# Summing the squares of the last two row blocks in halves, and sharing the closing waits between SP and Pool, in an eight-core decoder-trunk kernel

## The chip, the cores and the metric

The kernel runs on all eight cores of one Trainium2 chip (two dies: cores 0 to 3 and 4 to 7), each with its own share of the batch. The metric is the device time of the slowest core, in microseconds (us).

The runs fall into two states. In the fast one all cores are granted nearly the full TensorE clock (0.994 to 0.999 here). In the slow one a die gets less (cores at 0.813 to 0.972 in the slow runs below) and its cores take longer (in the run of squares_only at 1580.22, cores 0 to 3 have 0.861 to 0.879 and take 1559.3 to 1578.6 us, cores 4 to 7 have 0.996 to 0.998 and take 1404.3 to 1408.8).

## The reference

One step of a two-layer decoder trunk. Only its end matters here: the second MLP's output is added to the residual x, and the sum is normalised over its 1024 columns, row by row.

```python
def rmsnorm(x, g):
    xf = x.astype(jnp.float32)
    r = xf * lax.rsqrt(jnp.mean(xf * xf, axis=-1, keepdims=True) + EPS)
    return (r * g.astype(jnp.float32)).astype(x.dtype)
# in trunk(), after the last layer:
#   x = x + jnp.square(jax.nn.relu(h @ ff_w1[l])) @ ff_w2[l]
#   return rmsnorm(x, norm_final), ...
```

## The kernel before

A core holds 2048 rows as 16 row blocks of 128 rows (one row per partition) by 1024 columns. A Python scheduler emits every instruction: generators ("threads") yield operations, and the one that can start earliest goes next; waits between engines follow from the buffers read and written. `ACT(...)` makes a ScalarE activation, `STT` a VectorE scale-and-multiply, `DMA("sp", ...)` a store issued by SP.

The second MLP's output comes from a seven-product (Strassen-like) scheme, on quadrants of two row blocks by two column halves. The last such group handles row blocks 11 and 15. Its results are added to x in the order g (the right halves of both blocks), 11 (left half of block 11), 22 (right half of block 15), 12 (right half of 11), 21 (left half of 15). When a block has had its three additions, its normalisation is started:

```python
            for r in rows:
                b = 4 * (t0 + r) + j
                left[r] -= 1
                if left[r] == 0 and last:
                    if p == pairs[-1]:
                        S.spawn(norm(b, n_out, ("h%d" % n_out, b)), FINPRIO if n_out == 4 else NPRIO)
# ... cut ...
def norm(b, n, done):
    # ... cut: a scratch row ("junk"), and three columns ss, lt, rs of nrm ...
    yield ACT(junk, xb, AF.Square, [Bx], Bj + Bn, accum=ss)          # sum of 1024 squares
    yield ACT(lt, ss, AF.Ln, Bn, Bn, scale=1.0 / 1024, bias=EPS)
    yield ACT(rs, lt, AF.Exp, Bn, Bn, scale=-0.5)                    # 1/sqrt(mean + EPS)
    if n == 4:                                                       # the final norm
        yield up("gfin")
        if b in (14,):
            yield up("lastadd")                  # block 14 waits until the last addition is emitted
        for o, w in ((0, 512), (512, 512)) if b in (11, 15) else ((0, 1024),):
            q = slice(o, o + w)
            # ... cut ...
            yield STT(xb[:, q], xb[:, q], rs, hg[:, q], ALU.mult, ALU.mult, Bq + [Bn, B_hg], Bq)
            # ... cut ...
            yield DMA("sp", xy_ds[b if o == 0 else b - 8], [(yp[b][:, q], x_sb[:, b, q])], Bq, (), 512 * w)
        return
```

So blocks 11 and 15 are squared whole, but scaled and stored in halves of 256 KB. Block 14 is scaled and stored whole, 512 KB. At the end SP waits once for every DMA semaphore that was used (51 of them), in the order in which the scheduler thinks they are met; then all engines meet at the exit (in before between 1410.0 and 1410.2 us):

```python
final_waits = [(d.h, d.count) for d in sorted(P.dsems, key=lambda d: d.t) if d.count > 0]

def make_body(name, final=False):
    def body(eng):
        # ... cut: the engine's own stream ...
        if final:
            for h_, v_ in final_waits:
                eng.wait_ge(h_, v_)
    return body

block.sync(make_body("sp", final=True))
block.gpsimd(make_body("pool"))
```

## Time and profile before

| | before |
|---|---|
| median of the three runs given | 1470.35 us (1411.27 to 1488.31) |
| its fast run | 1411.27 us |
| profiled execution (fast), slowest core | 1410.2 us; all cores 1404.1 to 1410.2 |
| last matmul to the end of the program | 9.18 us on each of the eight cores |

From the page of before (its slowest core, 0): the span; busy time, share of the span and instruction count of each engine; the chain that ended last, by engine.

```profile
span 1410.2 us, 25622 instructions; the slowest of 8 cores (1404.1 to 1410.2 us)
...
PE 1367.9 (97%) x9123; PEld 694.2 (49%) x9145; DVE 1129.6 (80%) x2006; ACT 906.3 (64%) x1825; POOL 185.0 (13%) x265
...
PE 78%; DVE 10%; ACT 6%; DMA 3%; issue 2%; DVEq 0%; SPq 0%; ACTq 0%; POOLq 0%
```

TensorE bounds the kernel (97% of the span, 78% of the chain that ended last). The change touches nothing until the last group of products, so it has to be read in the last ten microseconds. That stretch is the timeline of before (core 0): start, duration, engine, line, operation, out<-in, shapes, count; in brackets the idle time before it and what ended it.

```profile
1399.89 1.88 DVE L564 TENSOR_TENSOR x_sb<-x_sb,pp 128x512 f32<-128x512 f32 x3
...
1400.00 1.02 PE L612 MATMUL pp<-mixT,arena 128*128 128x512 f16 x4
1401.27 1.06 ACT L530 ACTIVATE mixT<-x_sb 128x1024 f16<-128x1024 f32 x1 [1.06 <-DVE x_sb L564]
1401.69 1.28 DVE L582 SCALAR_TENSOR_TENSOR x_sb<-x_sb,nrm,hg 128x1024 f32<-128x1024 f32 x1
1402.23 0.19 ACT L530 ACTIVATION_READ_ACCUMULATOR mixT<-x_sb 128x1 f32 x1
1402.32 1.04 ACT L530 ACTIVATE mixT<-x_sb 128x1024 f16<-128x1024 f32 x1
1403.27 0.19 ACT L530 ACTIVATION_READ_ACCUMULATOR mixT<-x_sb 128x1 f32 x1
1403.36 0.75 ACT L529 ACTIVATE nrm<-nrm 128x1 f32<-128x1 f32 x4
1403.82 2.74 DVE L582 SCALAR_TENSOR_TENSOR x_sb<-x_sb,nrm,hg 128x512 f32<-128x512 f32 x4 [0.85 <-ACT nrm L529]
```

Read it downwards. The last matmuls end at 1401.02 and three additions (22, 12, 21) follow on DVE. ACT had been idle for 1.06 us when it began the first whole square; two squares and four one-column operations then take it to 1404.11. The 1.28 us DVE item in the middle is block 14's scaling; after it DVE idles 0.85 us for ACT, then scales four half rows until 1406.56.

What SP does after its last store (issued at 1406.69, landed at 1408.82) is on no chain in the profile, because waits are not busy time. It shows when one asks for the instructions of the source line of the closing waits (line, engine, count, durations in ns, first and last start):

```profile
L2561 SPq EVENT_SEMAPHORE  x51: 17/17/17, 1407.1 to 1409.9; - x51
```

An instruction takes 17 ns, but 51 of them take 2.88 us: in the trace one starts every 0.05 us, and one takes 0.37. The last is over at 1409.95, 1.13 us after the last landing, and the program ends at 1410.21.

The third thing to read is the store traffic. This is the DMA view of before over 6.00 us that begin 1.60 us after the last matmul (1402.62 to 1408.62): each digit is the busy share of the 16 DMA engines in 0.15 us, in tenths; then the stores with size and median time from issue to landing.

```profile
DMA  0000000049999999910599989999999999989710
...
yp<-x_sb SPq DMA_DIRECT2D x4, 256.0 KB, 2.2
yp<-x_sb SPq DMA_DIRECT2D x1, 512.0 KB, 2.6
```

Block 14's store fills the engines for 1.4 us, a gap of about two digits follows, then the four half-row stores come without a break.

### The profile page before, as it was taken

To read this page: it belongs to the slowest core of one execution; us is meant where nothing else is said; L and a number is where in the kernel's file an instruction comes from. 1 tells how busy PE (TensorE), PEld (TensorE's weight loads), DVE (VectorE), ACT (ScalarE), POOL (GpSimd) and SP (SyncE) were. 2 spreads that over 40 slices of the span, in tenths; PEclk is the share of its full clock that TensorE was granted. 3 is DMA by queue.
4 is the path that set the end of the run, shared out by engine and by line. 5 is a ranking of instruction groups with operands and counts; after the bars stand their busy time and mean duration, and the time that the engine had idled before them with its cause. 6 is when DMAs were issued, how large, how long until landed. Compare 5 with 4: busy or idle time off the path is not lost.

```text
span 1410.2 us, 25622 instructions; the slowest of 8 cores (1404.1 to 1410.2 us)
## 1 busy us (share of the span) xinstructions
PE 1367.9 (97%) x9123; PEld 694.2 (49%) x9145; DVE 1129.6 (80%) x2006; ACT 906.3 (64%) x1825; POOL 185.0 (13%) x265
## 2 busy tenths in 40 slices
PE   7999999999999999999999999999999999999997
PEld 3666655654454444454444444444444544444442
DVE  5897898886687788877778788999768778877777
ACT  5877878874465756854654765466747747745655
POOL 1221134333210110110100000000100100100100
PEclk9999999999999999999999999999999999999999
DMA  8672443397645964865845643630834625754613
GB/s 185 171 127 41 106 112 93 95 205 156 159 82 109 154 109 97 152 114 90 155 93 144 192 154 132 164 71 10 147 60 86 107 45 104 166 106 76 120 30 120
DMA packets 72473, 163.43 MB, mean 116 GB/s; under 512 B 6479, under 2 KB 36398, under 8 KB 72350
## 3 DMA queue, kind: packets, MB, share of 16 engines
q0 software_dynamic: 26960, 90.75, 39.0%
q1 hardware_dynamic: 45246, 70.98, 15.4%
q8 instruction: 76, 1.25, 0.4%
q14 instruction: 47, 0.39, 0.1%
q10 hardware_dynamic: 144, 0.07, 0.0%
HBM read 226.02 MB, written 26.55 MB: 179 GB/s over the span
## 4 chain that ended last, share of the span: by engine, by line
PE 78%; DVE 10%; ACT 6%; DMA 3%; issue 2%; DVEq 0%; SPq 0%; ACTq 0%; POOLq 0%
PE pp L612 40%; PE pp L614 37%; ACT arena L529 3%; DVE mixT L564 2%; PE pp L626 1%; DVE arena L564 1%; ACT pp L529 1%; DMA ring<-w2w 1%; DMA x_sb<-xp 1%; DVE x_sb L564 1%; DVE arena L582 1%; DVE hT L564 1%; DVE x_sb L570 1%; DVE arena L1845 1%; DMA ring<-wst 1%
## 5 line engine op out<-in xcount | busy, mean ns | idle before, releaser
L529 ACT ACTIVATE pp<-pp 128x512 f32<-128x512 f32 x456 | 260.0, 582 | 287.8 <-PE pp L612 194.5
L564 DVE TENSOR_TENSOR x_sb<-x_sb,pp 128x512 f32<-128x512 f32 (+1 forms) x392 | 293.8, 778 | 93.8 <-ACT pp L529 41.7
L614 PE MATMUL pp<-hT,ring 128*128 128x512 f16 (+1 forms) x1460 | 253.4, 311 | 4.5 <-DMA ring<-wst 1.7
L529 ACT ACTIVATE arena<-arena 128x512 f16<-128x512 f16 (+1 forms) x285 | 173.8, 625 | 23.9 <-DVE arena L1845 15.3
L529 ACT ACTIVATE arena<-pp 128x512 f32<-128x512 f32 (+2 forms) x224 | 131.1, 588 | 50.2 <-PE pp L614 29.3
L614 PEld LDWEIGHTS pp<-hT,ring 128*128 128x128 f16 x1460 | 108.9, 97 | 110.3 <-issue 9.5
L612 PE MATMUL pp<-hT,ring 128*128 128x512 f16 x648 | 159.9, 379 | 1.3 <-ACT pp L529 1.1
L612 PE MATMUL pp<-ring,arena 128*128 128x512 f16 x512 | 130.5, 379 | 0.8 <-ACT pp L529 0.8
L612 PEld LDWEIGHTS pp<-hT,ring 128*128 128x128 f16 x648 | 62.2, 98 | 77.1 <-issue 5.6
L614 PE MATMUL pp<-ring,mixT 128*128 128x512 f16 x416 | 96.8, 379 | 1.3 <-DVE mixT L564 1.2
L612 PE MATMUL pp<-mixT,arena 128*128 128x512 f16 x368 | 92.6, 379 | 0.0
L1845 DVE CUSTOM_DVE_ANT_0 arena<-pp,ring 128x512 f16<-128x512 f32 x106 | 70.1, 686 | 24.7 <-ACT pp L529 15.0
L612 PEld LDWEIGHTS pp<-ring,arena 128*128 128x128 f16 x512 | 49.5, 98 | 60.0 <-issue 1.9
L530 ACT ACTIVATE arena<-x_sb 128x1024 f16<-128x1024 f32 x56 | 59.0, 1054 | 21.6 <-DVE x_sb L564 18.2
L564 DVE TENSOR_TENSOR arena<-arena 128x1024 f16<-128x1024 f16 (+2 forms) x100 | 62.7, 648 | 11.1 <-ACT arena L529 10.2
L614 PE MATMUL pp<-ring,hT 128*128 128x128 f16 (+2 forms) x960 | 66.7, 226 | 0.1
L612 PE MATMUL pp<-mixT 128*128 128x512 f16 x240 | 61.6, 379 | 3.9 <-ACT pp L529 3.9
L529 ACT ACTIVATE x_sb<-x_sb 128x512 f32<-128x512 f32 (+3 forms) x98 | 54.1, 559 | 14.1 <-DVE x_sb L564 10.2
L614 PEld LDWEIGHTS pp<-ring,hT 128*128 128x128 f16 (+1 forms) x960 | 60.0, 97 | 5.4 <-issue 0.5
L614 PE MATMUL pp<-mixT,arena 128*128 128x512 f16 x240 | 61.4, 379 | 0.7 <-DVE arena L564 0.7
L612 PE MATMUL pp<-ring 128*128 128x512 f16 x240 | 61.6, 379 | 0.0
L612 PE MATMUL pp<-hT,mixT 128*128 128x512 f16 x240 | 61.6, 379 | 0.0
(266 smaller groups left out, 2312.7 us busy)
## 6 DMA issues: line engine op xcount, KB each, us to landing
ring<-w2w POOLq DMA_DIRECT2D x50, 512.0 KB, 8.4
ring<-w1w POOLq DMA_DIRECT2D x45, 512.0 KB, 8.6
ring<-wsc SPq DMA_DIRECT2D x24, 896.0 KB, 5.8
ring<-wst POOLq DMA_DIRECT2D x41, 512.0 KB, 8.6
x_sb<-xp SPq DMA_DIRECT2D x28, 512.0 KB, 5.7
extra<-w1w POOLq DMA_DIRECT2D x15, 512.0 KB, 7.8
yp<-x_sb SPq DMA_DIRECT2D x14, 512.0 KB, 2.8
x_sb<-st_hgrn SPq DMA_DIRECT2D x24, 256.0 KB, 4.3
```

Source lines behind the costliest of these rows:

```text
L529: return e.activation(out=out, in_=in_, func=func, bias=bias, scale=scale)
L530: return e.activation(out=out, in_=in_, func=func, bias=bias, scale=scale, accum_out=accum)
L564: return Op(eng, lambda e: e.tensor_tensor(out=out, in0=in0, in1=in1, op=op), R, W, *span(0.066, 0.15, n, two))
L570: return Op(eng, lambda e: e.tensor_tensor(out=out, in0=in0, in1=in1, op=op), R, W, occ, occ + 0.08)
L582: return Op("dve", lambda e: e.scalar_tensor_tensor(out=out, in0=in0, scalar=scalar, in1=in1, op0=op0, op1=op1), R, W, *(span(0.068, 0.218 ...
L612: ins = e.matmul(o, l, r, start=s, stop=t, skip_group_check=True)
L614: ins = e.matmul(o, l, r, start=s, stop=t)
L626: ins = e.transpose(out=o, in_=i, identity=idn)
L1845: yield Op("dve", lambda e: e._custom_dve(TENSOR_ADD_SAT, out=v, in0=bank(k), in1=gst(n), s0=3e38, s1=0.0), [B_ps[k], B_gst[n % 2]], B, 0. ...
```

## The change

Two ideas for the close. (1) Each of blocks 11 and 15 has one half complete early (11 after product "11", 15 after "22"). Its squares can be summed then, in time in which ACT is idle; only the other half remains after the last additions. The first half's sum, already divided by 1024 and with EPS added, becomes the bias of the later Ln. (2) SP keeps only the nine waits for the DMA semaphores expected last; Pool, which has no work left by then (in before its last issue ends at 1356.55), takes the other 42.

```diff
+NEND = 9
-        def norm(b, n, done):
+        def norm(b, n, done, parts=None):
 ...
-            yield ACT(junk, xb, AF.Square, [Bx], Bj + Bn, accum=ss)
-            yield ACT(lt, ss, AF.Ln, Bn, Bn, scale=1.0 / 1024, bias=EPS)
+            bias = EPS
+            if parts is not None:
+                bias = nrm[:, 4 * k + 3:4 * k + 4]
+                q = slice(parts * 512, parts * 512 + 512)
+                yield ACT(junk[:, q], xb[:, q], AF.Square, [Bx[parts]], Bj + Bn, accum=ss)
+                yield ACT(bias, ss, AF.Copy, Bn, Bn, scale=1.0 / 1024, bias=EPS)
+                yield up(("xsum", b))
+                q = slice(512 - parts * 512, 1024 - parts * 512)
+                yield ACT(junk[:, q], xb[:, q], AF.Square, [Bx[1 - parts]], Bj + Bn, accum=ss)
+            else:
+                yield ACT(junk, xb, AF.Square, [Bx], Bj + Bn, accum=ss)
+            yield ACT(lt, ss, AF.Ln, Bn, Bn, scale=1.0 / 1024, bias=bias)
             yield ACT(rs, lt, AF.Exp, Bn, Bn, scale=-0.5)
 ...
+                            end = last and n_out == 4 and p == pairs[-1] and j == 3
+                            if end and what in ("11", "22"):
+                                S.spawn(norm(b, n_out, None, h), FINPRIO)
 ...
-                                if left[r] == 0 and last:
+                                if left[r] == 0 and end:
+                                    flags.add(("xsum", b))
+                                elif left[r] == 0 and last:
 ...
-        final_waits = [(d.h, d.count) for d in sorted(P.dsems, key=lambda d: d.t) if d.count > 0]
+        used_sems = sorted((d for d in P.dsems if d.count > 0), key=lambda d: d.t)
+        final_waits = {"pool": used_sems[:-NEND], "sp": used_sems[-NEND:]}
 ...
-                if final:
-                    for h_, v_ in final_waits:
-                        eng.wait_ge(h_, v_)
+                for d in final_waits.get(name, ()):
+                    eng.wait_ge(d.h, d.count)
```

More of the change, by code (lines that the diff above doesn't have):

```diff
@@ L2541, in build, with make_body @@
         S.run()
-        final_waits = [(d.h, d.count) for d in sorted(P.dsems, key=lambda d: d.t) if d.count > 0]
-        def make_body(name, final=False):
+        used_sems = sorted((d for d in P.dsems if d.count > 0), key=lambda d: d.t)
+        final_waits = {"pool": used_sems[:-NEND], "sp": used_sems[-NEND:]}
+        def make_body(name):
             def body(eng):
@@ L2558, in body @@
                         ins.then_inc(P.esem[name], 1)
-                if final:
-                    for h_, v_ in final_waits:
-                        eng.wait_ge(h_, v_)
+                for d in final_waits.get(name, ()):
+                    eng.wait_ge(d.h, d.count)
             return body
-        block.sync(make_body("sp", final=True))
+        block.sync(make_body("sp"))
         block.scalar(make_body("act"))
```

## The prediction

> **What bounds the kernel now.** TensorE: busy 97% of the 1410.2 us span, 78% of the chain that ended last (the page). The change touches only the close. On every core the last matmul ends 9.18 us before the program (timelines). Slowest core, us from the span's start:
>
> - 1401.02 last matmul; the last adds end at 1400.58 (22), 1401.17 (12), 1401.77 (21).
> - ACT squares row block 11 whole (1401.27, 1.06 us), then 15 (1402.32, 1.04); the last Exp ends at 1404.11.
> - DVE's four half-row scalings start at 1403.82, every 0.66 us, and end at 1406.56.
> - SP's last store: issued 1406.69, landed 1408.82.
> - From 1407.07 to 1409.95 SP runs 51 closing waits, one per 0.05 us (one takes 0.37). The program ends at 1410.21, 0.26 us after the last wait and 1.39 us after the last landing (eight cores: 1.24 to 1.41).
>
> **Closing waits.** SP keeps nine; Pool, idle since 1356, takes 42, whose latest landing is at about 1391. SP then needs 9 x 0.05 = 0.45 us (estimate), done before the last landing. After the landing remain one wait's reaction and the 0.26 us exit: 0.31 instead of 1.24 to 1.41. Gain **0.95 to 1.1 us**, all critical: the list of waits outlasts the transfer beside it. [...]
>
> **Squares in halves.** For each of two row blocks two 128x512 squares replace one whole, with one more accumulator read and a 128x1 copy (about 0.19 us each, as the trace's Ln). [...] The first halves mostly go into ACT's 1.06 us of idle before 1401.27. After the add at 1401.17 ACT has two halves to do, not two wholes, plus copies: the first scaling starts 0.5 to 0.9 us earlier (DVE is busy with block 14 until 1402.9).
>
> **But the stores eat most of it.** A half-row store (256 KB) keeps the 16 DMA engines busy for 0.70 us, and scalings come every 0.66: the DMA view shows the engines full from 1405.6 to 1408.3. Block 14's store before them (1403.93 to 1405.35) doesn't move, as its scaling waits for the last add. Between it and the first half-row store the engines idle only 0.32 us: the last landing comes **about 0.3 us** earlier.
>
> **Total: 1.3 us** (0.9 to 1.7): last matmul to end 9.18 -> about 7.9; span 1410.2 -> about 1408.9; fast state 1411.3 -> **1410.0 us**. Fast runs should fall in 1406 to 1414. Two of the three runs before were slow (1470, 1488); a median may be slow again, so the range on record, 1406 to 1480, spans both. Chances: faster 0.01, same 0.97, slower 0.02.
>
> **Right or wrong in the profile.** Right: nine waits end SP; the end follows the last landing by about 0.3 us; first scaling 0.5 to 0.9 us earlier against the last matmul, last landing only 0.3; no DMA idle between the last five stores. Wrong: the landing moves as far as the scaling (stores not the limit), or not at all.
>
> **What would make it wrong.** The first half-square delays the PSUM copy that the last product waits for (1399.28), delaying the last matmul; the extra copies' waits on their own engine eat the ACT gain; Pool's waits or exit come last.

The sum: 0.95 to 1.1 us from the closing waits and about 0.3 us from the landing, 1.3 us in all (0.9 to 1.7). In after a half square takes 0.61 to 0.63 us of ACT.

## The result, and the profile after

Ratios here are the mean time of one kernel's fast runs over that of the other's of the same rounds, so they are not quite the ratios of the medians beside them.

| | before | after |
|---|---|---|
| runs | 1470.35, 1488.31, 1411.27, 1411.23 | 1410.80, 1409.99, 1409.41, 1410.93 |
| median of all | 1440.81 us | 1410.39 us |
| states | two slow, two fast | all fast |
| ratio of fast runs | | 0.9993, 95% interval 0.9969 to 1.0017: same |
| last matmul to end, eight cores | 9.18 (all) | 7.74 to 8.02, median 7.79 us |

The timeline of after (slowest core, now core 4, last matmul at 1401.45):

```profile
1400.31 0.61 ACT L531 ACTIVATE mixT<-x_sb 128x512 f16<-128x512 f32 x1
1400.31 1.88 DVE L565 TENSOR_TENSOR x_sb<-x_sb,pp 128x512 f32<-128x512 f32 x3
...
1400.43 1.02 PE L613 MATMUL pp<-mixT,arena 128*128 128x512 f16 x4
...
1401.09 0.63 ACT L531 ACTIVATE mixT<-x_sb 128x512 f16<-128x512 f32 x1
1401.63 0.19 ACT L531 ACTIVATION_READ_ACCUMULATOR mixT<-x_sb 128x1 f32 x1
1401.72 0.19 ACT L530 ACTIVATE nrm<-nrm 128x1 f32<-128x1 f32 x1
1402.00 0.63 ACT L531 ACTIVATE mixT<-x_sb 128x512 f16<-128x512 f32 x1
...
1402.96 0.61 ACT L531 ACTIVATE mixT<-x_sb 128x512 f16<-128x512 f32 x1
...
1403.79 2.74 DVE L583 SCALAR_TENSOR_TENSOR x_sb<-x_sb,nrm,hg 128x512 f32<-128x512 f32 x4 [0.40 <-ACT nrm L530]
```

Four half squares now. The first (1400.31) and the second (1401.09), with block 14's Exp moved between them (1400.92), fill what was idle time: the second ends 0.27 us after the last matmul, and before's idle ended 0.25 after it. The third starts at 1402.00, although its addition ended at 1401.60: the small copy at 1401.72, which empties the sum's column, stands before it. DVE's wait before the scalings fell from 0.85 to 0.40 us, and they start 2.34 us after the last matmul (1403.79 - 1401.45), not 2.79 (1403.82 - 1401.02).

The closing waits of after, and its DMA view over the same 6.00 us counted from its own last matmul (1403.05 to 1409.05):

```profile
L2577 POOLq EVENT_SEMAPHORE  x42: 17/17/17, 1356.4 to 1391.2; - x42
L2577 SPq EVENT_SEMAPHORE  x9: 17/17/17, 1407.0 to 1408.9; - x9
```

```profile
DMA  0000000049999999988999899989998999970000
...
yp<-x_sb SPq DMA_DIRECT2D x4, 256.0 KB, 2.3
yp<-x_sb SPq DMA_DIRECT2D x1, 512.0 KB, 2.9
```

Pool is done with its 42 waits at 1391, long before the end. SP's last three waits now really wait, each for a store to land: the ninth passes at 1408.92, when the last store lands (1408.90), and the program ends at 1409.19. The gap between block 14's store and the half-row stores is gone. The train starts in the same digit and ends about two digits earlier, less than the scalings' 0.45 us: the stores queue (2.3 and 2.9 us to landing, before 2.2 and 2.6).

### The profile page after: what moved, and what is told of

Same layout as the page of the kernel before. It is cut to its first block, busy times and chain, and to the rows that moved or that the text cites. A ratio compares the mean times of both kernels' runs of the same rounds, so it can differ in the third digit from the quotient of the medians.

```text
span 1409.2 us, 25632 instructions; the slowest of 8 cores (1402.6 to 1409.2 us)
## 1 busy us (share of the span) xinstructions
PE 1368.0 (97%) x9123; PEld 694.1 (49%) x9145; DVE 1128.9 (80%) x2006; ACT 906.5 (64%) x1831; POOL 185.1 (13%) x265
## 4 chain that ended last, share of the span: by engine, by line
PE 80%; DVE 10%; ACT 5%; DMA 2%; issue 2%; DVEq 0%; SPq 0%; POOL 0%; ACTq 0%; POOLq 0%
PE pp L613 40%; PE pp L615 38%; ACT arena L530 3%; DVE mixT L565 2%; PE pp L627 1%; DVE arena L565 1%; ACT pp L530 1%; DVE x_sb L565 1%; DMA ring<-wst 1%; DVE arena L583 1%; DVE hT L565 1%; DVE x_sb L571 1%; DVE x_sb L583 1%; DMA x_sb<-xp 1%; DVE arena L1856 1%
## 5 line engine op out<-in xcount | busy, mean ns | idle before, releaser
L613 PE MATMUL pp<-mixT 128*128 128x512 f16 x240 | 61.6, 379 | 3.7 <-ACT pp L530 3.7
L615 PE MATMUL pp<-mixT 128*128 128x512 f16 x240 | 61.6, 379 | 0.0
```

What stands on the lines that cost most here:

```text
L613: ins = e.matmul(o, l, r, start=s, stop=t, skip_group_check=True)
L615: ins = e.matmul(o, l, r, start=s, stop=t)
```

## The experiments

For a change of about 1 us the whole time is a poor measure: fast runs of one kernel spread over 1 to 3 us (after_again 1410.03 to 1411.50, before beside after_again 1411.71 to 1414.40). So I measured from the last matmul to four later events in each profile. The issue times repeat to 0.02 us over cores and runs. Landings differ between the two cores of a pair (0 and 1, 2 and 3, 4 and 5, 6 and 7): in every profile here, the core of a pair with the longer span (the slower core; the slowest of them sets the time) landed sooner relative to its last matmul (in after 7.45 to 7.52 us against 7.49 to 7.73). "Landing" and "end" in this table are medians over the slower core of each pair; the median of all eight cores, which the expectations speak of, is in brackets. Why the two differ was not tested.

| us after the last matmul | first scaling of 11 | last issue | last landing | end |
|---|---|---|---|---|
| before | 2.79 | 5.67 | 7.78 (7.84) | 9.18 (9.18) |
| close_only | 2.79 | 5.67 | 7.77 (7.87) | 8.06 (8.16) |
| squares_only | 2.34 | 5.21 | 7.46 (7.48) | 8.73 (8.73) |
| after | 2.34 | 5.21 | 7.47 (7.50) | 7.76 (7.79) |
| after_again | 2.34 | 5.21 | 7.49 (7.53) | 7.78 (7.82) |
| keep30 | 2.34 | 5.21 | 7.47 (7.49) | 7.76 (7.78) |
| keep45 | 2.34 | 5.21 | 7.46 (7.53) | 8.43 (8.43) |
| nocopy | 2.09 | 4.96 | 7.47 (7.48) | 7.76 (7.77) |
| split14 | 2.34 | 5.21 | 7.32 (7.34) | 7.61 (7.63) |
| both | 2.09 | 4.96 | 7.08 (7.21) | 7.37 (7.50) |

All eight runs gave correct results, and all profiles are of the fast state. The first four ran on one chip, the second four on another. Two questions: does the end follow the later of landing and list of waits (against: gains simply add up, wait by wait)? And do the stores limit the landing (against: the landing follows the scalings at a fixed distance)?

### close_only: the waits shared, the squares whole

```diff
 # before, with this part of the change alone
+used_sems = sorted((d for d in P.dsems if d.count > 0), key=lambda d: d.t)
+final_waits = {"pool": used_sems[:-NEND], "sp": used_sems[-NEND:]}
```

> Before with the closing waits alone split (SP keeps nine, Pool takes the rest); the squares stay whole. Measured from the last matmul to the end of the program, which was 9.18 us on all eight cores before and 7.74 to 8.02 after. My theory (the end is the later of two chains beside each other, the last store's landing and SP's list of waits): the last landing stays where it was before, 7.60 to 7.94 us after the last matmul by core (7.80 on the slowest), and the end follows 0.29 us after it: 8.05 to 8.25. Rival (the halved squares bring nearly all of the gain, the list hides under the transfer): 9.0 to 9.2. Whole time: 0.07% against before, not to be told from noise; slow runs, if any, fall on either kernel.

Measured: scaling, issue and landing as before; the end on the eight cores 8.05 to 8.27 us after the last matmul, 0.29 after the landing. The closing alone brings 0.91 to 1.13 us. (The expectation has a slip: the cores of before land at 7.77 to 7.94, not 7.60 to 7.94. Those of close_only land at 7.76 to 7.98, and so the latest end is 0.02 over the range expected.) Its source line shows why (slowest core): nine waits on SP, the last of them at the landing.

```profile
L2562 SPq EVENT_SEMAPHORE  x9: 17/17/17, 1406.7 to 1408.4; - x9
```

Whole time: ratio 0.9991, interval 0.9976 to 1.0006, same (medians 1409.99 against 1411.71, all 4 and 7 runs fast).

### squares_only: the squares in halves, the old closing

```diff
 # after, with SP waiting 51 times again
-final_waits = {"pool": used_sems[:-NEND], "sp": used_sems[-NEND:]}
+final_waits = [(d.h, d.count) for d in sorted(P.dsems, key=lambda d: d.t) if d.count > 0]
```

> After with the old closing: SP alone waits 51 times. My theory: the scalings and the last store's issue come 0.45 us earlier than before, as in after, the last landing only about 0.34 earlier; but the list of waits runs from the issue, so here the end follows the issue: 0.45 us earlier than before, 9.18 -> 8.73. So the two halves of the change, 1.0 and 0.45 apart, bring less than their sum together (1.16 to 1.44 by core). Rival (parts add, each acts on the landing): end 0.34 earlier, 8.84. Second rival (halves do nothing): 9.18.

Measured: 8.72 to 8.74 on all cores, as the list theory said; the additive rival's 8.84 is out. The end came 0.45 us earlier, the landing 0.32 (over all eight 0.36, by the table). The whole gain of the issue (0.46 by the table) passed on to the end, because SP's list starts at the issue and outlasts the landing (slowest core: landing at 1408.10):

```profile
L2576 SPq EVENT_SEMAPHORE  x51: 17/17/17, 1406.2 to 1409.1; - x51
```

So the parts are worth 1.12 and 0.45 alone and 1.42 together (all from the table): once the closing is shared, the half squares add 0.30. Of its four runs two were slow (1580.22 and 1540.12, one die at a clock of 0.861 to 0.912); its fast runs took 1410.95 and 1410.79.

### keep30 and keep45: how many waits are free

```diff
-NEND = 9
+NEND = 30        # keep45: 45
```

> After with 30 waits left to SP instead of nine. My theory: 30 x 0.05 = 1.5 us of waits start 0.38 us after the last issue and are done before the landing 2.2 to 2.5 us after it: last matmul to end as in after, 7.74 to 8.02 us, 0.29 us after the landing. Rival (each wait that SP keeps costs its share of the gain, 1.05 us / 42 = 0.025 us): 0.5 us more than after, about 8.3.

> After with 45 waits left to SP. My theory: 45 x 0.05 = 2.25 us, with the one slow wait seen before (0.37) 2.6, plus 0.38 ahead of it: SP is done 2.6 to 3.0 us after the last issue, later than the landing (2.2 to 2.5). End 8.1 to 8.4 us after the last matmul, the same on every core, not tied to the landing. Rival (0.025 us for each wait): 0.9 us more than after, 8.6 to 8.9.

The source lines, slowest core of each, keep30 first:

```profile
L2577 SPq EVENT_SEMAPHORE  x30: 17/17/17, 1406.3 to 1408.2; - x30
```

```profile
L2577 SPq EVENT_SEMAPHORE  x45: 17/17/17, 1407.4 to 1409.9; - x45
```

Thirty waits cost nothing: end at 7.74 to 8.01, as with nine. Forty-five end at 8.43 on every core, within 0.01 us and not tied to the landing (7.46 to 7.71); that is 0.03 above the range I gave (8.1 to 8.4). From 51 waits (squares_only, 8.73) to 45 the end moved by 0.30 us, 0.05 per wait; from 30 to 9, by nothing. The linear rivals (8.3, and 8.6 to 8.9) are out. The number nine is not critical.

### nocopy, split14 and both: what holds the last landing

after_again is the changed kernel once more, as their base on the same chip.

> The changed kernel itself once more, beside the kernel before on one chip, as the base of the three runs below. First scaling 2.34 us after the last matmul, last issue 5.21, last landing 7.49 (median of eight cores, 7.45 to 7.73), end 7.78. Whole time of fast runs: 0.9990 to 0.9995 of before, 1.3 us, about as much as runs of one kernel differ (1410.6 to 1412.1).

Its medians repeated the first profile within 0.03 us. Its ratio to before is 0.9991 (0.9978 to 1.0003), all six of its runs fast; of before's eleven runs there, three were slow.

nocopy takes the small copies out of ACT's path. With them goes EPS (1e-6) in blocks 11 and 15: nocopy and both are probes, not replacements as they stand.

```diff
-yield ACT(junk[:, q], xb[:, q], AF.Square, [Bx[parts]], Bj + Bn, accum=ss)
-yield ACT(bias, ss, AF.Copy, Bn, Bn, scale=1.0 / 1024, bias=EPS)
+yield ACT(junk[:, q], xb[:, q], AF.Square, [Bx[parts]], Bj + Bn, scale=1.0 / 32, accum=bias)
 ...
-yield ACT(junk[:, q], xb[:, q], AF.Square, [Bx[1 - parts]], Bj + Bn, accum=ss)
+yield ACT(junk[:, q], xb[:, q], AF.Square, [Bx[1 - parts]], Bj + Bn, scale=1.0 / 32, accum=ss)
 ...
-yield ACT(lt, ss, AF.Ln, Bn, Bn, scale=1.0 / 1024, bias=bias)
+yield ACT(lt, ss, AF.Ln, Bn, Bn, scale=1.0 / 1024 if parts is None else 1.0, bias=bias)
```

> After without the two small copies: each half is squared with scale 1/32, so its sum comes out divided by 1024, and the first half's sum is Ln's bias as it stands (the 1e-6 inside the root is left out, harmless here). The copy of block 11 held up its second half by 0.28 us in after. Both theories: first scaling and last issue about 0.28 us earlier (2.06 and 4.93). My theory (the train of stores behind block 14's is the next limit; it is full already): the last landing moves by 0 to 0.06 us, median 7.43 to 7.49. Rival (scalings set the landing, the stores follow 2.2 us behind): 7.20 to 7.25.

split14 lets the train of stores start earlier:

```diff
-for o, w in ((0, 512), (512, 512)) if b in (11, 15) else ((0, 1024),):
+for o, w in ((0, 512), (512, 512)) if b in (11, 14, 15) else ((0, 1024),):
```

> After with block 14 scaled and stored in two halves as well, so that the train of stores starts about 0.5 us earlier (0.66 less some overhead) with the same bytes. First scaling of block 11 and last issue stay (2.34, 5.21, at most 0.1 later). My theory: the stores stop being the limit, the last landing follows the last issue by 2.13 as in an empty queue: median 7.34 to 7.40, 0.1 to 0.15 earlier. Rival (scalings alone set it): 7.49, unmoved.

(The 2.13 is the last store of before's slowest core, 1406.69 to 1408.82. The first half-row store there, before whose packets the engines fall idle for about two digits, took 2.21 us; on the slower cores of the pairs such a first store took 2.10 to 2.21.)

both has the two edits together.

> nocopy and split14 together. First scaling about 2.06 to 2.1, last issue 4.93 to 5.0. My theory: each removes the limit that hid the other, so the landing moves by more than the sum of the two alone: median 7.08 to 7.18, 0.3 to 0.4 earlier than after, and the end at 7.37 to 7.47. Rival: as nocopy alone, 7.20 to 7.25 (if nocopy moved it at all). Whole time: 0.3 to 0.4 us below after, 1.7 below before, 0.9988; not to be told from after by runs.

Measured (table): in nocopy the scalings and the last issue came 0.25 us earlier, and the landing did not move: 7.47 against 7.47 and 7.49 (all eight: 7.48 against 7.50 and 7.53). The rival needed 7.20 to 7.25. In split14 nothing moved on ACT, and the last issue stayed, but the landing came 0.15 us earlier. With both it came 0.39 us earlier, more than the 0.00 and 0.15 alone. Over all eight cores that excess is smaller: 0.29 to 0.32 earlier with both, against a sum of 0.18 to 0.24 for the two alone (against after and after_again). Over all eight cores the landing of both is 7.21 and its end 7.50 (expected 7.37 to 7.47): the landing is just outside my 7.08 to 7.18 and inside the rival's 7.20 to 7.25. What refutes the rival is nocopy, and four of both's cores (7.06 to 7.09); its other four, all the faster cores of their pairs, land at 7.33 to 7.42.

The DMA views show the trade, over the same 6.00 us after the last matmul (slowest core of each, here core 7 three times). nocopy:

```profile
DMA  0000000068999999989999999999999999960000
...
yp<-x_sb SPq DMA_DIRECT2D x4, 256.0 KB, 2.5
yp<-x_sb SPq DMA_DIRECT2D x1, 512.0 KB, 2.7
```

split14:

```profile
DMA  0000079999999930599999999999999899610000
...
yp<-x_sb SPq DMA_DIRECT2D x6, 256.0 KB, 2.1
```

both:

```profile
DMA  0000079999999969999999999999999992000000
...
yp<-x_sb SPq DMA_DIRECT2D x6, 256.0 KB, 2.1
```

In nocopy the train is as full as in after, and the half-row stores queue longer (2.5 us, after 2.3). In split14 it starts three digits earlier, but a gap opens again in front of block 11, for ACT is not ready (DVE waits 0.28 us for it): the scalings limit. In both the start is early and the gap is nearly closed.

both has the shortest close: 0.39 to 0.41 us less than after from the last matmul to the end (0.29 to 0.32 over all eight cores). By its runs it cannot be told from after: ratio to before 0.9987 (0.9975 to 1.0000), five fast runs of 1409.74 to 1411.71, and one slow of 1661.32 with a die at a clock of 0.813 to 0.829.

## Why the prediction was right or wrong

**The number: wrong as a forecast of a change.** The text derives a gain of 1.3 us, "fast state 1411.3 -> **1410.0 us**". As a fast-state time this was right (1410.39 measured). But the record set a fast 1410.0 against a time before that was given as 1470.35, which is mostly slow runs. Read against that, it forecasts 60 us or 4.1% less, while the text's own chances say 0.97 for no change. Measured between fast runs, the change is 0.07% (repeat: 0.09%). The step that failed is therefore the last one, "a median may be slow again, so the range on record, 1406 to 1480, spans both": I treated the state as an uncertainty of the result only, and did not carry it back to the time I was comparing with. A consistent forecast was either 1411.3 -> 1410.0, said to be fast against fast, or 1470.35 less 1.3, about 1469. A range of 74 us for an effect of 1.3 also said nothing about the effect.

What the runs show in its place: the state belongs to the execution. Of the 22 runs of before, 5 were slow; of squares_only 2 of 4, of both 1 of 6, of close_only none of 4, of after none of 10. Slow runs occurred with and without either part of the change, so neither part removes them. None of 10 against 5 of 22 is what chance gives 13 times in 100 (the hypergeometric share, C(22,5)/C(32,5)), so whether after is less prone to it stays open; nothing in the traces suggests so. That the medians of all runs fell by 30 us (1440.81 to 1410.39) is thus, as far as the runs show, the luck of which executions were slow.

**"Closing waits ... 0.31 instead of 1.24 to 1.41. Gain 0.95 to 1.1 us": right.** 0.29 us on all eight cores of after; close_only gained 0.91 to 1.13. keep30 and keep45 show the reason given, two chains side by side.

**"The first scaling starts 0.5 to 0.9 us earlier": slightly over.** It was 0.45. The mis-sized term is the copies. I counted their time but not their place: block 11's copy has to clear the sum's column before the second half may use it, and this copy with the wait for it took ACT from 1401.72 to 1402.00, 0.28 us in the middle of its path. nocopy gives 0.70 us (2.79 - 2.09), the middle of what I had put. The prediction had named this among what could go wrong.

**"The last landing comes about 0.3 us earlier", the stores eat the rest: right.** 0.31 us on the slower cores, 0.34 over all eight. At 0.45 us the ACT gain and the stores' limit lie close together, so after alone could not have shown it. nocopy does: 0.25 us more from ACT and nothing at the landing. split14 and both show which store was the limit.

**"Last matmul to end 9.18 -> about 7.9": right**, 7.79 (median of eight). The half squares did not delay the PSUM copy that the last product waits for: the first of them starts at 1400.31, after that copy (1399.71), and from the copy's start to the last matmul's end it is 1.74 us in both traces.

## What to carry to other kernels

When a program ends, list what runs side by side after its last compute, here the last transfer and a list of waits: in these runs only the longer one cost, and shortening it beyond the other brought nothing (from 51 waits to 45 the end moved by 0.30 us, from 30 to 9 by nothing). Before making the producer of back-to-back stores faster, compare its step (0.66 us) with how long a store occupies the DMA engines (0.70 us: from 1405.50 to 1408.50 the engines of before were 94% busy, 2.82 us for four half-row stores): where the engines are full, look at the start of the train instead. Here scalings 0.25 us earlier moved the landing by 0.00 to 0.02 us (nocopy), and an earlier start of the train by 0.15 (split14). And predict a change in the state in which the time before was taken; if that is a median over two states, say which one your number is for.

## Further measurements of the close

- The closing list is serial and follows the last issue: in before its first wait starts 0.38 us after SP's last store is issued, each met wait takes 0.05 us, and the 51 take 2.88 us. From the last wait to the end of the program it is 0.26 us, on all eight cores of before and of after.
- The one slow wait: the 43rd on SP took 0.37 us in before, squares_only and keep45, on all eight cores (the lists of the last two, 51 waits from 1406.2 to 1409.1 and 45 from 1407.4 to 1409.9, have the length that 0.05 us each and one such wait give). In keep45 the 43rd waits for another semaphore than in the other two, so it goes with the place in the list or the time since its start, not with the semaphore; the cause was not tested.
- Four 512 KB stores of before (core 0, issued at 1393.34 to 1403.10, with packets that overlap no other store) have their first packet 0.83 us after the issuing instruction starts and 0.50 us after it ends, then about 1.43 us of packets, and land 0.35 to 0.49 us after the last packet.
